# The output projection of a hybrid decoder layer as seven half products, with VectorE alone at the merge and the squares of x1 issued behind the MLP's third column tile

## Chip, cores and metric

One Trainium2 chip, one of its cores. The metric is the device time of one execution in microseconds (us), lower being better. Before the change it is 905.8 us, the median of three runs (905.01 to 906.35). "Engines" are TensorE (PE, with its weight loads as PEld), VectorE (DVE), ScalarE (ACT), GpSimd (POOL) and SyncE (SP), whose queue issues the loads.

## What is computed

One layer for 512 tokens and a width of 1024, all in float32: a chunkwise mLSTM branch (y_a) and a sliding-window attention branch (y_b) on one normalised input, merged by gates, projected and added to x, then an MLP with a squared relu and a gated embedding of the layer's own. The change lies in these lines of the reference:

```python
merged = jax.nn.sigmoid(g_a) * (y_a @ w_branch_a[i]) + jax.nn.sigmoid(g_b) * (y_b @ w_branch_b[i])
x = x + merged @ w_out[i]

u = rmsnorm(x, norm_mlp_g[i]) @ w_up[i]
x = x + jnp.square(jax.nn.relu(u)) @ w_down[i]
```

## The kernel before

**Products.** Every float32 operand is split into a high part (a cast on ACT, L134) and a low part (a subtraction on VectorE, L135; L137 and L138 for columns with a scale), and a product is three matmuls: high with high, high with low, low with high. `chain` (L162) issues them. Weights come by `load_w`: a raw tile of 128x1024 from a ring of four (`wr`), split into rings of four `wh` and `wl`.

**Merge (L846 on).** For each of 8 tiles of 128 columns, TensorE runs 24 matmuls of 128x512 over y_a into a slot `psg` (a ring of two); VectorE multiplies by the gate (L850, `sga`); GpSimd adds the other branch (L851, `gb`); ACT and VectorE split the sum into `mg`. The gates (`gl`) come from DRAM, where an earlier stage has put them, through the SP queue like the weights.

**Output projection (L864 to L897).** The PSUM pool of the first half of the kernel is closed, and a new one (`pq`: three tiles `psp` of two banks, two `psg` of one) is opened; x is loaded into `xk`. For each half of 512 output columns, four loads of w_out with 4 x 6 matmuls each accumulate 128 tokens x 512 columns in four banks: 2 x 96 = 192 matmuls of 128x512. VectorE adds the banks to x (L895). Then `columns_of` (L877) transposes the result x1 in 128x128 pieces, four to a column tile k of 8, and splits each with a scale: this is what the MLP multiplies.

**MLP.** The squares of x1's rows (ACT, L916) and a factor from them (VectorE, L917 and L918) stand in the code ahead of it; the factor is used only when a down product is added to x. An up tile (`up`) is 24 matmuls of 128x512 into `psg`, a relu (L937) and a square (L941) on ACT. A down projection (`down`) already runs as seven half products with sums of quarters, 168 matmuls of 128x512.

A scheduler orders the instructions of each engine from the order of the code and its own costs; on each engine they run in that fixed order, and an instruction that waits holds all that stand behind it on its engine. A tile's next user waits until the earlier users of its slot are done.

Of the kernel before, what the change touches and what calls it, by code (L numbers as in the profile page):

```python
# [22 lines left out]
NEG = -1e30  # L23
NH = 4
DV = 256
# [5 lines left out]
WRB = 4  # L31
LOOK = 2
LMB = 4
# [3 lines left out]
def block_kernel(  # L37
# [39 lines left out]
    wp = pool(ctx, "wp")  # L77
    bp = pool(ctx, "bp")
    ap = pool(st_a, "ap")
    c1 = pool(st_s, "c1", side="right")  # L80
    sp = pool(st_s, "sp", side="right")
    pp = pool(st_p, "pp", space=PSUM)
# [28 lines left out]
    def act_hl(n="s"):  # L111
        return [act_r(n), act_r(n)]

    def big_hl(n):

        hl = [bp.tile([P, KT, 512], F32R, tag="big", bufs=2, name=nm(n)) for _ in range(2)]
        return hl, [[t[:, k, :] for t in hl] for k in range(KT)]

    def tk(n):
        return sp.tile([P, NH * (DV + 1)], F32, tag="tk", bufs=4, name=nm(n))  # L120

    def tok_scratch(n="lm"):
        return sp.tile([P, D], F32, tag="lm", bufs=LMB, name=nm(n))
# [1 line left out]
    def small(n, w, bufs=4):  # L125
        return cp.tile([P, w], F32, tag=f"{n}{w}", bufs=bufs, name=nm(n))
# [4 lines left out]
    def split(dst, src, scale=None):  # L131

        if scale is None:
            A.copy(dst[0], src)  # L134
            V.tensor_sub(dst[1], src, r32(dst[0]))  # L135
        else:
            A.activation(dst[0], src, AF.Copy, scale=scale)  # L137
            V.scalar_tensor_tensor(dst[1], src, scale, r32(dst[0]), ALU.mult, ALU.subtract)  # L138
# [54 lines left out]
    ident = cp.tile([P, P], F32, name="ident")  # L193
# [648 lines left out]
    ya_of(3)  # L842


    mg = []
    for i in range(8):  # L846
        ps = ps_g()
        mm_T(ps, load_w(w_a[i], KT * P, KT), ya)
        sg = act_f("sga")
        V.tensor_mul(sg, ps, gate_of(gad, i))  # L850
        G.tensor_tensor(sg, sg, t2[i], ALU.add)  # L851
        m_ = act_hl("mg")
        split(m_, sg)
        mg.append(m_)


    st_s.close()
    st_p.close()
    xp = pool(ctx, "xp", side="right")
    pp = pool(ctx, "pq", space=PSUM)  # L860
    XK = xp.tile([P, NT, D], F32, name="xk")
    xk = [XK[:, m, :] for m in range(NT)]
    for m in range(NT):
        nc.sync.dma_start(out=xk[m], in_=x[m * P : (m + 1) * P, :])  # L864

    def pair():

        return pp.tile([P, 2, 512], F32, tag="pair", bufs=3, name=nm("psp"))

    def ps_g():  # L870
        return pp.tile([P, 512], F32, tag="g", bufs=2, name=nm("psg"))

    def columns_of(dst, k, g):

        ps = pair()[:, 0, :]
        for m in range(NT):
            T.transpose(ps[:, m * P : (m + 1) * P], xk[m][:, k * P : (k + 1) * P], ident)  # L877
        split(dst[k], ps, g[:, k : k + 1])


    x1b, x1 = big_hl("x1")
    for nh in range(2):
        if nh == 0:
            a, b = pair(), pair()
            pv = [a[:, 0, :], a[:, 1, :], b[:, 0, :], b[:, 1, :]]
        else:
            a = pair()
            pv = [a[:, 0, :], a[:, 1, :], ps_g(), ps_g()]
        for c in range(4):
            w = load_w(w_out[nh * 4 + c], 2 * 512, 2)  # L890
            for m in range(NT):
                mm_tok(pv[m], w, mg[2 * c : 2 * c + 2], m, first=c == 0, last=c == 3)
        for m in range(NT):
            o = xk[m][:, nh * 512 : (nh + 1) * 512]
            V.tensor_add(o, pv[m], o)  # L895
        for k in range(4):
            columns_of(x1, 4 * nh + k, gmlp)  # L897

# [9 lines left out]


    r2 = cp.tile([P, NT], F32, name="r2")
    for m in range(NT):
        junk = np_.tile([P, 7 * 256], F32, tag="uf", bufs=8, name=nm("junk"))[:, :D]
        ss = small("ss", 1)
        A.activation(junk, xk[m], AF.Square, accum_out=ss)  # L916
        V.tensor_scalar(ss, ss, 1.0 / D, EPS, ALU.mult, ALU.add)  # L917
        V.reciprocal(r2[:, m : m + 1], ss)  # L918

    def load_down(q):  # L920
        raws = []
# [9 lines left out]
    def up(q, uf):  # L931
        fs = None
        for f in range(8):
            ps = ps_g()
            mm_T(ps, load_w(w_up[q * 8 + f], KT * P, KT), x1)
            a = mp.tile([P, 512], F32, tag="rt", bufs=3, name=nm("rt"))
            A.activation(a, ps, AF.Relu)  # L937
            if f % 2 == 0:
                fs = F()
            o = 2 * (f % 2)  # L940
            A.activation(fs[:, o : o + 2, :].rearrange("p a b -> p (a b)"), a, AF.Square)  # L941
            if f % 2:
                hl = [np_.tile([P, 7 * 256], F32R, tag="uf", bufs=8, name=nm("uf")) for _ in range(2)]

                cut = 3 * 256 if f == 7 else 0
                if cut:
                    split([t[:, :cut] for t in hl], fs[:, 1:4, :].rearrange("p a b -> p (a b)"))
                V.tensor_add(fs[:, S1, :], fs[:, A21, :], fs[:, A22, :])
                V.tensor_sub(fs[:, S3, :], fs[:, A11, :], fs[:, A21, :])
                V.tensor_sub(fs[:, S2, :], fs[:, S1, :], fs[:, A11, :])  # L950
                V.tensor_sub(fs[:, S4, :], fs[:, A12, :], fs[:, S2, :])  # L951
                split([t[:, cut:] for t in hl], fs[:, 1 + cut // 256 :, :].rearrange("p a b -> p (a b)"))
                uf.append(hl)
# [102 lines left out]

    x2b, x2 = big_hl("x2")
    for k in range(4):
        columns_of(x2, k, gple)
    ple(0, wp0)  # L1060
    for k in range(4, 8):
        columns_of(x2, k, gple)
    evicted = ple(1, load_w(w_pp[1], 2 * 512, 2))
    rk = []
    fs = cp.tile([P, NT, 4], F32, name="fs")
# [113 lines left out]
def _quarters(w):  # L1179


    return w.reshape(2, 2, 2, P, 2, 512).transpose(0, 2, 4, 3, 1, 5).reshape(8, P, 1024)
# [12 lines left out]
def _layout(i):  # L1195
    w = i["w_in"][0]
    down = i["w_down"][0]
    return {
        "x": i["x"][0],
        "p": i["p"][0, 0],  # L1200
        "w_qkml": _t_form(w[:, 0:1024]),
        "w_vml": _quarters(w[:, 1024:2048]).reshape(2, 4, P, 1024).transpose(1, 0, 2, 3).reshape(8, P, 1024),
        "w_o": _t_form(w[:, 2048:3072]),
        "w_vsif": _tok_form(np.concatenate([w[:, 4360:4616], w[:, 3072:3080]], axis=1), KT, 264)[0],
        "w_qsw": _t_form(_heads(w[:, 3080:4104])),
        "w_ksw": _t_form(w[:, 4104:4360]),
        "w_ga": _halves(w[:, 4616:5640]),
        "w_gb": _halves(w[:, 5640:6664]),
        "w_a": _t_form(i["w_branch_a"][0]),
        "w_b": _t_form(_heads(i["w_branch_b"][0].T).T),  # L1210
        "w_out": _tok_form(i["w_out"][0], 2, 512),
        "w_up": _t_form(i["w_up"][0]),
        "w_down": np.concatenate([_quarters(down[q * 1024 : (q + 1) * 1024]) for q in range(4)], axis=0),
        "w_pg": _tok_form(i["w_ple_gate"][0], 2, 512),
        "w_pp": _tok_form(i["w_ple_proj"][0], 2, 512),
        "g_mix": i["norm_mix_g"],
        "g_ml": _columns(i["mlstm_norm_g"][0]),
        "g_mlp": _columns(i["norm_mlp_g"][0]),
        "g_ple": _columns(i["norm_ple_g"][0]),
        "g_fin": i["final_norm_g"][None, :],  # L1220
        "conv": i["conv_qk"][0].reshape(4, KT, P).transpose(2, 1, 0).reshape(P, KT * 4),
        "b_if": i["b_if"],
        "sinks": i["sinks"],
    }
# [19 lines left out]
```

## Time and profile before

| | us |
|---|---|
| median of three runs | 905.8 |
| the profiled run | 905.84 |
| its span | 904.1 |
| TensorE busy | 890.4 |
| VectorE busy | 627.0 |
| ScalarE busy | 466.9 |
| GpSimd busy | 28.1 |

The span is what the trace covers; the rest of the run, 1.7 us, lies outside. Rows of the trace read: start, length, engine, line, operation, out<-in by the program's names without their numbers, form, count, and in brackets the idle time of the engine just before with what ended it. A row of groups gives count, busy us, mean ns of one and the idle time before. Matmuls overlap, so the length of one is more than the step from one to the next.

### The profile page before, as it was taken

Reading aid. Unit: us, or ns where it says so; the run is one execution under the profiler, and the core shown is the slowest. Engines: PE = TensorE matmul, PEld = TensorE weight load, DVE = VectorE, ACT = ScalarE, POOL = GpSimd, SP = SyncE. Lnnn points to the kernel's source line nnn. Section 1 sums busy time; section 2 is a strip of 40 time slices with the busy share of each in tenths; the row PEclk is TensorE's granted clock in tenths of the full one; section 3 lists DMA queues with packets and bytes.
Section 4 is the critical chain, followed back from the end, with each engine's and each line's share of the span. In section 5 each row is a group of like instructions: output and inputs, shape, how many; then the busy total and the mean of one; then the engine's idle time right before and its main releaser. Section 6 shows DMA issues by size and latency. Waiting matters only on the chain.

```text
span 904.1 us, 11781 instructions
## 1 busy us (share of the span) xinstructions
PE 890.4 (98%) x4500; PEld 741.6 (82%) x4500; DVE 627.0 (69%) x1016; ACT 466.9 (52%) x778; POOL 28.1 (3%) x47
## 2 busy tenths in 40 slices
PE   8999999999999999999999999999999999999996
PEld 7888899998877677777878888888888888888786
DVE  6884687874787977557644568856965795689556
ACT  6473444443676667664322555345535543554753
POOL 2021000000000000001210000000000000000000
PEclk9999999999999999999999999999999999999999
DMA  7753134435121132234452620631262044101402
GB/s 259 252 159 125 47 116 157 149 122 168 61 70 52 43 117 71 94 103 150 144 187 94 228 74 2 209 119 45 68 212 94 1 162 161 49 24 50 160 1 94
DMA packets 30347, 101.52 MB, mean 112 GB/s; under 512 B 4301, under 2 KB 4813, under 8 KB 30290
## 3 DMA queue, kind: packets, MB, share of 16 engines
q1 hardware_dynamic: 28002, 93.15, 31.0%
q0 software_dynamic: 2144, 7.35, 2.3%
q8 instruction: 35, 0.57, 0.3%
q10 hardware_dynamic: 144, 0.26, 0.1%
q14 instruction: 22, 0.18, 0.1%
HBM read 91.30 MB, written 8.40 MB: 110 GB/s over the span
## 4 chain that ended last, share of the span: by engine, by line
PE 73%; ACT 2%; DVE 2%; DMA 1%; issue 0%; SPq 0%; ACTq 0%
PE psg L162 42%; PE psp L162 22%; PE pst L784 2%; PE pst L713 1%; PE psa L705 1%; PE pst L774 1%; PE psa L162 1%; PE psa L668 1%; PE psa L669 1%; DMA gfin<-in_g_fin 1%; PE psp L877 1%; ACT jk L796 1%; ACT wh L134 1%; ACT pT L707 0%; DMA ptok<-in_p 0%
## 5 line engine op out<-in xcount | busy, mean ns | idle before, releaser
L135 DVE TENSOR_TENSOR wl<-wr,wh 128x1024 fp32r<-128x1024 f32 x134 | 170.7, 1279 | 131.0 <-ACT wh L134 124.4
L134 ACT CAST wh<-wr 128x1024 fp32r<-128x1024 f32 x134 | 140.9, 1053 | 208.5 <-PE psg L162 85.6
L162 PE MATMUL psg<-x,wh 128*128 128x512 f32 x512 | 157.9, 389 | 0.0
L162 PE MATMUL psp<-wh,uf 128*128 128x512 f32 x448 | 139.2, 390 | 0.0
L162 PEld LDWEIGHTS psg<-x,wh 128*128 128x128 f32 x512 | 96.0, 188 | 19.8
L162 PE MATMUL psg<-h,wh 128*128 128x512 f32 x320 | 101.3, 395 | 0.0
L162 PE MATMUL psg<-x,wl 128*128 128x512 f32 x256 | 99.6, 389 | 0.0
L162 PEld LDWEIGHTS psp<-wh,uf 128*128 128x128 f32 x448 | 84.1, 188 | 17.4
L162 PE MATMUL psp<-wl,uf 128*128 128x512 f32 x224 | 87.2, 390 | 0.0
L134 ACT CAST wh<-wd 128x1024 fp32r<-128x1024 f32 x44 | 46.3, 1055 | 60.4 <-PE psp L162 23.2
L162 PEld LDWEIGHTS psg<-h,wh 128*128 128x128 f32 x320 | 58.7, 188 | 15.9 <-issue 4.9
L135 DVE TENSOR_TENSOR wl<-wd,wh 128x1024 fp32r<-128x1024 f32 x44 | 53.3, 1220 | 17.6 <-ACT wh L134 17.4
L162 PE MATMUL psg<-h,wl 128*128 128x512 f32 x160 | 62.8, 393 | 0.0
L162 PEld LDWEIGHTS psg<-x,wl 128*128 128x128 f32 x256 | 48.1, 188 | 10.0
L162 PE MATMUL psa<-h,wh 128*128 128x256 f32 (+1 forms) x256 | 55.1, 311 | 0.2 <-ACT p L593 0.2
L162 PEld LDWEIGHTS psp<-wl,uf 128*128 128x128 f32 x224 | 42.0, 188 | 8.7
L135 DVE TENSOR_TENSOR uf<-F,uf 128x1792 fp32r<-128x1792 f32 (+2 forms) x20 | 33.0, 1652 | 21.8 <-ACT uf L134 21.8
L162 PEld LDWEIGHTS psa<-h,wh 128*128 128x128 f32 x256 | 41.8, 190 | 3.7 <-ACT p L593 0.9
L162 PE MATMUL psg<-yb,wh 128*128 128x512 f32 x128 | 42.7, 408 | 0.0
L162 PE MATMUL psg<-ya,wh 128*128 128x512 f32 x128 | 40.7, 394 | 0.0
L162 PE MATMUL psa<-h,wl 128*128 128x256 f32 (+1 forms) x128 | 39.6, 309 | 0.0
L134 ACT CAST uf<-F 128x1792 fp32r<-128x1792 f32 (+2 forms) x20 | 28.0, 1399 | 19.3 <-DVE F L951 19.2
(284 smaller groups left out, 1667.7 us busy)
## 6 DMA issues: line engine op xcount, KB each, us to landing
wr<-in_w_up SPq DMA_DIRECT2D x32, 512.0 KB, 3.2
wd<-in_w_down SPq DMA_DIRECT2D x24, 512.0 KB, 3.3
wr<-in_w_o SPq DMA_DIRECT2D x8, 512.0 KB, 4.8
gd<-gr POOLq DMA_DIRECT2D x8, 512.0 KB, 3.2
wr<-in_w_qsw SPq DMA_DIRECT2D x8, 512.0 KB, 4.0
wr<-in_w_qkml SPq DMA_DIRECT2D x8, 512.0 KB, 3.3
wr<-in_w_b SPq DMA_DIRECT2D x8, 512.0 KB, 3.2
gl<-gd SPq DMA_DIRECT2D x8, 512.0 KB, 3.4
```

The lines of the kernel that those rows point to most:

```text
L134: A.copy(dst[0], src)
L135: V.tensor_sub(dst[1], src, r32(dst[0]))
L162: last_mm[0] = T.matmul(ps, l, r, start=first and i == 0, stop=last and i == len(ops) - 1, skip_group_check=parts)
L668: T.matmul(o, q[:, n * P : (n + 1) * P], kk[kp][ab][:, k0 : k0 + 256], start=True, stop=False)
L669: T.matmul(o, q[:, n * P : (n + 1) * P], kl[kp][ab][:, k0 : k0 + 256], start=False, stop=True)
L705: T.transpose(pt[:, c : c + P], lm3[ab][:, g, j * P : (j + 1) * P], ident)
L713: T.matmul(o[HALF[ab], :], vs[n + 1 - nk + j][:, c : c + 64], pTs[j][:, ab * 512 : (ab + 1) * 512], start=j == 0, stop=j == nk - 1,)
L774: T.matmul(psc[:, n0:], qk[4 + h][:, n0 : n0 + P], qk[h][:, n0:], start=True, stop=True)
L784: T.matmul(pn[:, : DV + 1], wT[s][:, t * P : (t + 1) * P], vm[s][:, h, :], start=s == 0, stop=s == t)
L796: A.activation(jk[:, :DV], h_of(h, t), AF.Square, scale=rd[:, t : t + 1], accum_out=hss[:, h, t : t + 1])
L877: T.transpose(ps[:, m * P : (m + 1) * P], xk[m][:, k * P : (k + 1) * P], ident)
```

## The change

- **The matrix of merged columns is not used as it stands, but in quarters.** With the tokens cut into two halves of 256, and the merged columns into even and odd tiles, A11, A21, A12 and A22 are quarters of the merged matrix. For each pair of merge tiles VectorE forms S1 = A21 + A22, S2 = S1 - A11, S3 = A11 - A21, S4 = A12 - S2 (four sums of 128x256). Four tiles are split for each pair: A11 (128x256), A22 with A12, S1 with S2, S3 with S4 (128x512 each).
- **GpSimd's add of the merge is VectorE's** (`V.tensor_add`).
- **w_out is laid out in quarters** b11, b12, b21 and b22 of two tiles each, and VectorE forms their sums (8 operations of 128x1024). b11, b12 are loaded into buffers of the attention stage as these come free, b21 and b22 during the merge. x is loaded into four tiles that held another stage's values, as soon as these come free.
- **Seven half products** of 24 matmuls each: A11, S2, A12, S3, S1, A22, S4, into X and Y (two banks each, `psa`) and Z (two `pst`) of the first PSUM pool; the new pool is opened only afterwards. ACT copies X after A11 (`p_841`, `p_842`), since A11's product is added three times. VectorE makes 14 adds of 128x512 into `xk`, where 8 stood.
- **Columns of x1 come two to a tile** (`two_columns`), two pairs of them set between pieces of the last product.
- **The squares of x1** are issued behind the square of the third up tile.

Where the new order of VectorE differs in the merge: the three rows of each tile before (here two tiles: multiplication by the gate, weight's low part, merged tile's low part; `psg` is the product, `gl` the gate).

```order
L850 TENSOR_TENSOR sga_4097<-psg_4066,gl_4098 128x512
L135 TENSOR_TENSOR wl_4226<-wr_4223,wh_4225 128x1024
L135 TENSOR_TENSOR mg_4103<-sga_4097,mg_4102 128x512
L850 TENSOR_TENSOR sga_4137<-psg_4106,gl_4098 128x512
L135 TENSOR_TENSOR wl_4266<-wr_4263,wh_4265 128x1024
L135 TENSOR_TENSOR mg_4141<-sga_4137,mg_4140 128x512
```

After the change, VectorE between the first pair's adds and the multiplication of the third tile (`sga_4208`, the last row); `ms` holds S1 with S2 (4163) and S3 with S4 (4164), the `wq` sums are quarters of w_out.

```order
L136 TENSOR_TENSOR wl_4307<-wr_4304,wh_4306 128x1024
L136 TENSOR_TENSOR mg_4160<-sga_4152,mg_4159 128x512
L887 TENSOR_TENSOR ms_4163<-sga_4116,sga_4152 128x256
L932 TENSOR_TENSOR wq_4073<-wq_4449,wq_4073 128x1024
L888 TENSOR_TENSOR ms_4163<-ms_4163,sga_4116 128x256
L932 TENSOR_TENSOR wq_4075<-wq_4451,wq_4075 128x1024
L136 TENSOR_TENSOR mg_4168<-ms_4163,mg_4167 128x512
L892 TENSOR_TENSOR ms_4164<-sga_4116 128x256
L893 TENSOR_TENSOR ms_4164<-sga_4152,ms_4163 128x256
L136 TENSOR_TENSOR wl_4363<-wr_4360,wh_4362 128x1024
L136 TENSOR_TENSOR mg_4174<-ms_4164,mg_4173 128x512
L865 TENSOR_TENSOR sga_4208<-psg_4177,gl_4209 128x512
```

A multiplication that followed two rows behind the one of the tile before now stands behind the whole work of the first pair, and behind two weight sums that need loads of b22 (`wq_4449`, `wq_4451`).

ScalarE at the end of the merge after the change: casts of weights (`wh`) and of merged parts (`mg`), and the copies of X (`psa_4459`).

```order
L135 CAST wh_4537<-wq_4453 128x1024
L135 CAST mg_4431<-sga_4426 128x512
L135 CAST wh_4554<-wq_4455 128x1024
L135 CAST mg_4439<-ms_4435 128x512
L135 CAST wh_4573<-wq_4073 128x1024
L135 CAST mg_4445<-ms_4436 128x512
L938 COPY p_841_4499<-psa_4459 128x512
L938 COPY p_842_4500<-psa_4459 128x512
```

The two copies, which before has not, stand behind the cast of the last pair's S3 and S4 (`ms_4436`).

VectorE at the last columns of x1, before: the adds into `xk`, the factor (`ss`, `r`), and the low parts of the last four columns from four tiles `psp`.

```order
L895 TENSOR_TENSOR xk<-psg_4550,xk 128x512
L917 TENSOR_SCALAR ss_4713<-ss_4713 128x1
L918 RECIPROCAL r_4711<-ss_4713 128x1
L917 TENSOR_SCALAR ss_4718<-ss_4718 128x1
L918 RECIPROCAL r_4711<-ss_4718 128x1
L138 SCALAR_TENSOR_TENSOR x_800_4393<-psp_4675,gmlp,x_799_4392 128x512
L138 SCALAR_TENSOR_TENSOR x_800_4393<-psp_4682,gmlp,x_799_4392 128x512
L138 SCALAR_TENSOR_TENSOR x_800_4393<-psp_4689,gmlp,x_799_4392 128x512
```

After the change, the same place: all eight columns (k0, k2, k1, k3, k4, k6, k5, k7), the last two adds, and a weight split.

```order
L139 SCALAR_TENSOR_TENSOR x_832_4458<-psa_4703,gmlp,x_831_4457 128x512
L929 TENSOR_TENSOR xk_4079<-pst_4461,xk_4079 128x512
L139 SCALAR_TENSOR_TENSOR x_832_4458<-psa_4723,gmlp,x_831_4457 128x512
L929 TENSOR_TENSOR xk_4080<-pst_4462,xk_4080 128x512
L139 SCALAR_TENSOR_TENSOR x_832_4458<-psa_4703,gmlp,x_831_4457 128x512
L136 TENSOR_TENSOR wl_4920<-wr_4917,wh_4919 128x1024
L139 SCALAR_TENSOR_TENSOR x_832_4458<-psa_4723,gmlp,x_831_4457 128x512
L139 SCALAR_TENSOR_TENSOR x_832_4458<-psa_4743,gmlp,x_831_4457 128x512
L139 SCALAR_TENSOR_TENSOR x_832_4458<-psa_4756,gmlp,x_831_4457 128x512
L139 SCALAR_TENSOR_TENSOR x_832_4458<-psa_4743,gmlp,x_831_4457 128x512
L139 SCALAR_TENSOR_TENSOR x_832_4458<-psa_4756,gmlp,x_831_4457 128x512
```

Each tile `psa` now appears twice, once for each of its columns; the factor's rows are gone from here, and a weight split for the fourth up tile (`wl_4920`) stands between columns.

The diff, without the deletions of the old loops, which the kernel above shows:

```diff
+    b11 = [load_quarter(4 * kh, sp, "lm", LMB) for kh in range(2)]
+    b12 = [load_quarter(4 * kh + 1, sp, "lm", LMB) for kh in range(2)]
+    xk = [tk("xk")[:, :D] for _ in range(NT)]
+    for m in range(NT):
+        nc.sync.dma_start(out=xk[m], in_=x[m * P : (m + 1) * P, :])
+    def merged(i):
+        ps = ps_g()
+        mm_T(ps, load_w(w_a[i], KT * P, KT), ya)
+        sg = act_f("sga")
+        V.tensor_mul(sg, ps, gate_of(gad, i))
+        V.tensor_add(sg, sg, t2[i])
+        return sg
+    halves_of = lambda t: [t[:, :256], t[:, 256:]]
+    mf = []
+    for i in range(4):
+        even, odd = merged(2 * i), merged(2 * i + 1)
+        a21, a11 = halves_of(even)
+        a22, a12 = halves_of(odd)
...
+        split(part, a11)
...
+        split(hl, odd)
+        V.tensor_add(s1, a21, a22)
+        V.tensor_sub(s2, s1, a11)
...
+        split(hl, t12)
+        V.tensor_sub(s3, a11, a21)
+        V.tensor_sub(s4, a12, s2)
...
+        split(hl, t34)
+    b22 = [load_quarter(4 * kh + 3, wp, "wr", WRB) for kh in range(2)]
+    b21 = [load_quarter(4 * kh + 2, sp, "pT", 2) for kh in range(2)]
+    def halves_a():
+        t = ps_a()
+        return [t[:, :512], t[:, 512:]]
+    def out_proj():
+        X, Y, Z = halves_a(), halves_a(), [ps_t(), ps_t()]
...
+        for kh in range(2):
+            V.tensor_sub(b12[kh], b22[kh], b12[kh])
+        for kh in range(2):
+            prod(X, "A11", form(b11[kh]), kh, True, False)
+            V.tensor_add(b11[kh], b12[kh], b11[kh])
+        own = [act_f("p1") for _ in range(2)]
+        for t in range(2):
+            A.copy(own[t], X[t])
+        for kh in range(2):
+            prod(Y, "S2", form(b11[kh]), kh, True, False)
+        acc(Y, 1, 1)
+        for kh in range(2):
+            prod(X, "A12", form(b21[kh]), kh, False, True)
+            V.tensor_sub(b21[kh], b21[kh], b11[kh])
+        acc(X, 1, 0)
+        for kh in range(2):
+            prod(Y, "S3", form(b12[kh]), kh, False, False)
...
+        for kh in range(2):
+            V.tensor_sub(b11[kh], b22[kh], b11[kh])
+            prod(Z, "S1", form(b11[kh]), kh, True, False)
...
+        for kh in range(2):
+            prod(Y, "A22", form(b21[kh]), kh, False, True)
+        acc(Y, 0, 0)
+        w = [form(b22[kh]) for kh in range(2)]
+        prod(Z, "S4", w[0], 0, False, True)
+        two_columns(0)
+        prod(Z, "S4", w[1], 1, False, True, [0])
+        acc(Z, 1, 1, [0])
+        two_columns(2)
+        prod(Z, "S4", w[1], 1, False, True, [1])
+        acc(Z, 1, 1, [1])
+        two_columns(4)
+        two_columns(6)
+    def two_columns(k):
+        two = halves_a()
+        for i in range(2):
+            columns_of(x1, k + i, gmlp, two[i])
+    out_proj()
...
-    for m in range(NT):
-        junk = np_.tile([P, 7 * 256], F32, tag="uf", bufs=8, name=nm("junk"))[:, :D]
+    def norm_factor():
+        for m in range(NT):
...
-            A.activation(fs[:, o : o + 2, :].rearrange("p a b -> p (a b)"), a, AF.Square)
+            squared = A.activation(fs[:, o : o + 2, :].rearrange("p a b -> p (a b)"), a, AF.Square)
+            if (q, f) == (0, 2):
+                with tc.issue_after(squared.ins):
+                    norm_factor()
```

More of the change, by code (lines that the diff above doesn't have):

```diff
@@ L79, in block_kernel @@
     ap = pool(st_a, "ap")
+    xp = pool(ctx, "xp", side="right")
     c1 = pool(st_s, "c1", side="right")
@@ L119, in tk @@
     def tk(n):
-        return sp.tile([P, NH * (DV + 1)], F32, tag="tk", bufs=4, name=nm(n))
+        return xp.tile([P, NH * (DV + 1)], F32, tag="tk", bufs=4, name=nm(n))
     def tok_scratch(n="lm"):
@@ L842, in block_kernel, with load_quarter @@
     ya_of(3)
-    mg = []
-    for i in range(8):
+    def load_quarter(c, pool_, tag, bufs):
+        t = pool_.tile([P, 1024], F32, tag=tag, bufs=bufs, name=nm("wq"))
+        nc.sync.dma_start(out=t, in_=w_out[c])
+        return t
+    b11 = [load_quarter(4 * kh, sp, "lm", LMB) for kh in range(2)]
[4 more added lines that the diff above has]
+    def merged(i):
         ps = ps_g()
@@ L850, in block_kernel @@
         V.tensor_mul(sg, ps, gate_of(gad, i))
[L851 to L854, printed above, removed]
+        V.tensor_add(sg, sg, t2[i])
[6 more added lines that the diff above has]
+        a22, a12 = halves_of(odd)
+        if i % 2 == 0:
+            own = act_hl("mg")
+        part = [halves_of(t)[i % 2] for t in own]
+        split(part, a11)
+        f = {"A11": part}
+        hl = act_hl("mg")
+        split(hl, odd)
+        f["A22"], f["A12"] = zip(*[halves_of(t) for t in hl])
+        t12, t34 = act_f("ms"), act_f("ms")
+        s1, s2 = halves_of(t12)
+        s3, s4 = halves_of(t34)
+        V.tensor_add(s1, a21, a22)
+        V.tensor_sub(s2, s1, a11)
+        hl = act_hl("mg")
+        split(hl, t12)
+        f["S1"], f["S2"] = zip(*[halves_of(t) for t in hl])
+        V.tensor_sub(s3, a11, a21)
+        V.tensor_sub(s4, a12, s2)
+        hl = act_hl("mg")
+        split(hl, t34)
+        f["S3"], f["S4"] = zip(*[halves_of(t) for t in hl])
+        mf.append(f)
@@ new lines, in block_kernel, with columns_of, form, prod @@
+    b22 = [load_quarter(4 * kh + 3, wp, "wr", WRB) for kh in range(2)]
[3 more added lines that the diff above has]
+        return [t[:, :512], t[:, 512:]]
+    def columns_of(dst, k, g, ps):
+        for m in range(NT):
+            T.transpose(ps[:, m * P : (m + 1) * P], xk[m][:, k * P : (k + 1) * P], ident)
+        split(dst[k], ps, g[:, k : k + 1])
+    def out_proj():
+        X, Y, Z = halves_a(), halves_a(), [ps_t(), ps_t()]
+        def form(raw):
+            return load_w(None, 1024, 2, raw)
+        def prod(ps, a, w, kh, first, last, toks=range(2)):
+            for t in toks:
+                ops = []
+                for k in range(2):
+                    ops += pairs([h[:, t * P : (t + 1) * P] for h in mf[2 * kh + k][a]], [h[:, k, :] for h in w])
+                chain(ps[t], ops, first and kh == 0, last and kh == 1, True)
+        def acc(ps, toks, n, part=range(2)):
+            for t in part:
+                o = xk[2 * toks + t][:, n * 512 : (n + 1) * 512]
+                V.tensor_add(o, ps[t], o)
+        for kh in range(2):
[15 more added lines that the diff above has]
+            prod(Y, "S3", form(b12[kh]), kh, False, False)
+        acc(Y, 0, 1)
+        acc(own, 0, 1)
+        for kh in range(2):
+            V.tensor_sub(b11[kh], b22[kh], b11[kh])
+            prod(Z, "S1", form(b11[kh]), kh, True, False)
+        acc(Z, 0, 1)
+        acc(own, 1, 1)
+        acc(own, 0, 0)
+        for kh in range(2):
[11 more added lines that the diff above has]
+        two_columns(6)
@@ L857, in block_kernel @@
+    x1b, x1 = big_hl("x1")
+    def two_columns(k):
[3 more added lines that the diff above has]
+    out_proj()
     st_s.close()
     st_p.close()
-    xp = pool(ctx, "xp", side="right")
     pp = pool(ctx, "pq", space=PSUM)
-    XK = xp.tile([P, NT, D], F32, name="xk")
-    xk = [XK[:, m, :] for m in range(NT)]
-    for m in range(NT):
-        nc.sync.dma_start(out=xk[m], in_=x[m * P : (m + 1) * P, :])
     def pair():
@@ L871, in ps_g @@
         return pp.tile([P, 512], F32, tag="g", bufs=2, name=nm("psg"))
[L873 to L897, printed above, removed]
     st_a.close()
@@ L912, in block_kernel @@
     r2 = cp.tile([P, NT], F32, name="r2")
-    for m in range(NT):
-        junk = np_.tile([P, 7 * 256], F32, tag="uf", bufs=8, name=nm("junk"))[:, :D]
[L915 to L918, printed above, removed]
+    def norm_factor():
+        for m in range(NT):
+            junk = np_.tile([P, 7 * 256], F32, tag="uf", bufs=8, name=nm("junk"))[:, :D]
+            ss = small("ss", 1)
+            A.activation(junk, xk[m], AF.Square, accum_out=ss)
+            V.tensor_scalar(ss, ss, 1.0 / D, EPS, ALU.mult, ALU.add)
+            V.reciprocal(r2[:, m : m + 1], ss)
     def load_down(q):
@@ L1058, in block_kernel @@
     for k in range(4):
-        columns_of(x2, k, gple)
+        columns_of(x2, k, gple, pair()[:, 0, :])
     ple(0, wp0)
     for k in range(4, 8):
-        columns_of(x2, k, gple)
+        columns_of(x2, k, gple, pair()[:, 0, :])
     evicted = ple(1, load_w(w_pp[1], 2 * 512, 2))
@@ L1210, in _layout @@
         "w_b": _t_form(_heads(i["w_branch_b"][0].T).T),
-        "w_out": _tok_form(i["w_out"][0], 2, 512),
+        "w_out": _quarters(i["w_out"][0]),
         "w_up": _t_form(i["w_up"][0]),
```

## The prediction, made before the changed kernel ran

> **What bounds the kernel now.** The first view is the page's busy times with the line of granted clock, the second the chain of work that ended last, in order of time, around the change (columns: start, length, engine, what, how many).
>
> ```profile
> span 904.1 us, 11781 instructions
> PE 890.4 (98%) x4500; PEld 741.6 (82%) x4500; DVE 627.0 (69%) x1016; ACT 466.9 (52%) x778; POOL 28.1 (3%) x47
> PEclk9999999999999999999999999999999999999999
> ```
>
> ```profile
> 419.41 39.87 PE psg L162 x174
> 459.30 1.05 ACT wh L134
> 460.37 22.03 PE psp L162 x96
> 506.25 1.44 PE psp L877 x12
> 510.43 41.31 PE psg L162 x182
> 551.74 38.08 PE psp L162 x168
> 589.82 43.52 PE psg L162 x192
> ```
>
> TensorE is busy 98% of the span, and the chain runs along it: the merge to 459.3, one step of 1.05 us off it, then the output projection and the MLP. 192 matmuls of 128x512 take 43.52 us, so one is 0.2267 us. The 168 of a down projection take 38.08, the same 0.2267: seven products already run elsewhere in this kernel without a wait. So a matmul removed here is worth its full 0.2267, and each new wait of TensorE costs in full. The waits of TensorE from 410 to 760 show how little idle time there is to win:
>
> ```profile
> PE psp L162 <- ACT wh L134: 0.9, 1, 0.9
> ```
>
> **What goes.** 192 matmuls become 168: 24 x 0.2267 = 5.44 us. The wait between merge and projection goes too: the chain has it as 459.30 to 460.37, 1.07 us. There the new PSUM pool could not be written until VectorE had read the last merge tile; the row blames ACT, but the cast begins before that read ends. In the change the projection starts in slots of the old pool that have long been free, with weights already split. From 460.37 to 510.43 the chain holds 50.06 us, in which TensorE issues 202 matmuls (192 and ten of the first up tile) and 32 transposes. At 0.2267 and, by 1.44/12, 0.12 us, these make 49.6; some 0.5 is small gaps around transposes. I count the new tail gap by gap, so the 0.5 goes as well. Removed: 5.44 + 1.07 + 0.5 = 7.0 us.
>
> **What VectorE gets in the merge.** Groups of the merge by line, VectorE then GpSimd (columns: busy us, mean ns, idle before), and behind them single rows of VectorE and GpSimd.
>
> ```profile
> L135 DVE TENSOR_TENSOR wl<-wr,wh 128x1024 fp32r<-128x1024 f32 x8 | 16.3, 2038 | 1.1 <-ACT wh L134 1.1
> L850 DVE TENSOR_TENSOR sga<-psg,gl 128x512 f32<-128x512 f32 x8 | 5.5, 690 | 9.7 <-PE psg L162 9.7
> L851 POOL TENSOR_TENSOR sga<-sga,gb 128x512 f32<-128x512 f32 x7 | 9.9, 1419 | 238.3 <-ACT wh L134 223.5 <-DVE sga L850 14.8
> ```
>
> ```profile
> 454.91 1.28 POOL L851 TENSOR_TENSOR sga<-sga,gb 128x512 f32<-128x512 f32 x1 [4.20 <-ACT wh L134]
> 454.95 2.33 DVE L135 TENSOR_TENSOR wl<-wr,wh 128x1024 fp32r<-128x1024 f32 x1 [0.17 <-ACT wh L134]
> 457.20 0.68 DVE L135 TENSOR_TENSOR mg<-sga,mg 128x512 fp32r<-128x512 f32 x1
> 549.16 0.42 DVE L949 TENSOR_TENSOR F<-F 128x256 f32<-128x256 f32 x1
> 549.50 1.22 DVE L986 TENSOR_TENSOR wd<-wd,wd 128x1024 f32<-128x1024 f32 x1
> 558.23 1.22 DVE L997 TENSOR_TENSOR wd<-wd,wd 128x1024 f32<-128x1024 f32 x1
> 559.36 1.22 DVE L135 TENSOR_TENSOR wl<-wr,wh 128x1024 fp32r<-128x1024 f32 x1
> ```
>
> A 1024 wide subtraction takes 1.22 us, started every 1.13 to 1.14; a 512 wide one 0.68, every 0.60; a 256 wide one 0.42, every 0.34 (549.16 to 549.50). In the merge the 1024 wide one takes 2.04 on average, and the row of 2.33 begins together with GpSimd's add of 1.28. With that add gone I take 1.14. The other end is 2.04, in case the stage and not the add lengthens it; it makes the slower rival. [...]
>
> Between the merge's first multiplication and the last split of S3 and S4 the new order gives VectorE 8 multiplications, 8 adds and 12 splits of 512, four splits and 16 sums of 256, and 16 operations of 1024: 28 x 0.60 + 20 x 0.34 + 16 x 1.14 = 41.8 us, in the 46 or so from 423.7 to 470. VectorE is now 90% full there, and delays come from the order:
>
> - Merge tile 4 needs the PSUM slot of tile 2, whose multiplication stands behind all work of the first pair. Counting back from 459.30 in steps of 24 x 0.2267 = 5.44, tile 1 ends at 426.7 and tile 3 at 437.5. From 426.7 VectorE has a multiplication, two 512s, a 1024 and two 256s (3.7 us, to 430.4), then a weight sum with the first quarter of b22, a 256, and a sum that waits for the second quarter.
>
> ```profile
> 429.27 6.62 SPq L143 DMA_DIRECT2D wr<-in_w_out  x2
> wr<-in_w_out SPq DMA_DIRECT2D x8, 512.0 KB, 3.3
> xk<-in_x SPq DMA_DIRECT2D x4, 512.0 KB, 5.4
> ```
>
> That load is issued when the split at about 429.9 frees its buffer (before issues one at 429.27) and lands 3.3 us later, at 433.2. Behind it stand two 1024s, two 512s and two 256s, 4.2 us; tile 2's multiplication ends near 438.1, and tile 4 starts **0.7 late** (0 if the load lands a microsecond sooner; 2.8 if it takes x's 5.4).
> - A12 adds into the bank of A11, which ACT copies first. The copies stand behind the cast of S3 and S4 of the last pair. With tile 7 ending at 460.0, S2 ends at 470.9. VectorE's split of the first b21 waits for ACT's cast, and this for A11's first half: 464.0. From there three 1024s, two 512s and four 256s, 6.0 us, so S4 ends at 470.1; a cast of 0.62 and two copies of 0.59 (row below) later it is 471.9. **1.0 late**, with 0 to 2 as bounds. The other five products have their splits 0.1 us or more ahead.
>
> **The tail.** Columns of x1 now use a two-bank tile for two columns, and the second column's transposes wait for the first column's split. The rows show one round, near the kernel's end:
>
> ```profile
> 842.02 0.59 ACT L1054 COPY pe<-psg 128x512 f32<-128x512 f32 x1 [0.68 <-PE psg L162]
> 843.52 0.75 DVE L138 SCALAR_TENSOR_TENSOR x<-psp,gple,x 128x512 fp32r<-128x512 f32 x1
> 844.33 0.66 PE L877 MATMUL psp<-ident,xk 128*128 128x128 f32 x4 [0.54 <-DVE x L138]
> 845.02 0.69 ACT L137 ACTIVATE x<-psp,gple 128x512 fp32r<-128x512 f32 x1 [0.46 <-PE psp L877]
> 845.59 0.66 PE L877 MATMUL psp<-ident,xk 128*128 128x128 f32 x4 [0.60 <-DVE x L138]
> 846.28 0.69 ACT L137 ACTIVATE x<-psp,gple 128x512 fp32r<-128x512 f32 x1 [0.57 <-PE psp L877]
> 847.00 0.75 DVE L138 SCALAR_TENSOR_TENSOR x<-psp,gple,x 128x512 fp32r<-128x512 f32 x1 [0.16 <-ACT x L137]
> ```
>
> Transposes to ACT 0.69 (844.33 to 845.02), ACT to VectorE 0.72 (846.28 to 847.00), VectorE 0.75, and 0.06 until the next transposes (843.52 + 0.75 to 844.33): 2.2 us a round. With P the end of S4's first half, four transposes 0.45 and the matmuls in their places, the columns start at: k0 P, k2 1.8, k1 3.2, k3 4.1, none late. k4 needs k1's split, which VectorE does behind the last add of x: 5.7 instead of 4.5. Behind k1's split stands a weight split of 1024, whose cast also precedes ACT's half of k3, so k6 starts at 7.6, k5 at 8.2, k7 at 9.8, and the first up tile at 10.2. Without waits it would be 12 x 0.2267 + 32 x 0.113 = 6.3: **3.9 late**. Bounds: 1.7 if the weight split and the add were not in the way (two bare rounds), 6 if a second weight split came between. Nothing covers these 3.9: only transposes and the up tile behind them are left. Moving the squares of x behind the third up tile delays only ACT's next relu by some 4 us; its PSUM slot is needed 5.44 later, so I cost that at nothing, and a microsecond if the cover fails.
>
> **Sum.** 905.84 (the profiled run, 1.7 outside its span; the median is 905.8) - 7.0 + 0.7 + 1.0 + 3.9 = 904.4.
>
> **Rivals.**
> - *The tail hides.* The trace has rounds only where ACT and VectorE were nearly free; if the adds and weight split run earlier than I walk them, 1.7 or less is left: 902.2, or 900.5 with no tail wait. Against it: the order of the two queues is fixed.
> - *VectorE becomes the bound of the merge (slower).* The 41.8 us fill 46; the 16 long operations decide. Above 1.14 + 4.5/16 = 1.42 us each every further microsecond is TensorE's. At 1.65 (between 1.14 and 2.04) it is 3.7 more: 908.1; at 2.04, 914. For it: the mean of 2038 ns; against it: 1.22 wherever GpSimd rests.
> - *Loads collide.* x and half of w_out now come before and during the merge, when gates for the last columns of y_a are due:
>
> ```profile
> 415.00:420.00 5.00, 5.00 (x30) 4.18 (x28) 4.68 (x7) 1.66 (x3) 0.00 (x0) 1.00 0.91 313
> 840.00:845.00 5.00, 4.45 (x23) 3.33 (x21) 2.54 (x5) 3.10 (x6) 0.00 (x0) 1.00 0.89 324
> ```
>
> The share of DMA is 0.91 there already (the last two columns are share and GB/s, the one ahead the clock). A load at 5.4 instead of 3.3 would cost up to 2 us: 905.4 to 906.4. For the forecast: x is issued some six microseconds earlier.
> - *The clock drops in the tail.* At half clock the tail's 6.3 and the up tile's 5.4 double: 916. Against it: from 840 to 845 TensorE waits twice for rounds, and the clock stays 1.00. [...]
>
> **How the numbers follow.** Forecast 904.4 (902.9 to 906, tail from 2.4 to 5.5) 0.46; tail hidden 0.21; collision 0.09; VectorE bound 0.22; clock 0.02. A measurement of this kernel tells about 0.2% from no change, 1.8 us: faster is below 904.0, slower above 907.6. Of the forecast's 0.46, 0.18 lies below 904.0. Faster 0.18 + 0.21 = 0.39; same 0.28 + 0.09 = 0.37; slower 0.24. The range of 8 in 10 reaches from the hidden tail to VectorE's mid price: 900.5 to 908.5.
>
> **What would show it.** Right: 168 matmuls at 0.2267, 1024 wide splits in the merge at 1.22, TensorE waiting 0.7 on the multiplication at merge tile 4, 1.0 on ACT's copies, about 3.9 on splits of x1. Wrong: waits at every merge tile, a gate or quarter that lands late, more than one weight split between two columns, or waits in the first up tiles.

## The result, and the profile after

The changed kernel takes 907.94 us (median of 17 runs, 905.45 to 910.38) where the kernel before takes 905.24 (17 runs beside them, 904.39 to 906.37): a ratio of 1.0026, 95% interval 1.0019 to 1.0033. By that ratio it is slower by some 2.4 us. The time lies in the range of the prediction, but on the other side of the kernel before from the forecast of 904.4. That the range holds it is luck: its upper end was priced with VectorE as the bound of the merge, which did not happen.

The profiled run took 908.09 with a span of 906.3, 2.2 more than before. The page's busy times and its line of granted clock:

```profile
span 906.3 us, 11792 instructions
PE 887.3 (98%) x4476; PEld 737.4 (81%) x4476; DVE 654.2 (72%) x1072; ACT 476.8 (53%) x794; POOL 16.8 (2%) x39
PEclk9999999999999999999999899999999999999999
```

TensorE issues 24 matmuls fewer, but is busy only 3.1 us less, not 5.4, and one digit of the clock is an 8, which the page of before does not have: slice 23, 498 to 521 us. TensorE's waits from 410 to 760, and the chain around the change:

```profile
PE psa L909 <- DVE x L139: 2.5, 3, 1.1
PE psg L163 <- DVE sga L865: 1.7, 1, 1.7
PE pst L825 <- DVE sy L826: 0.6, 2, 0.4
PE psa L163 <- ACT p L938: 0.4, 1, 0.4
```

```profile
429.32 4.59 DMA wq<-in_w_out
438.92 22.04 PE psg L163 x96
494.67 2.74 PE pst L163 x12
504.81 1.13 PE psa L909 x4
508.61 45.03 PE psg L163 x192
553.63 38.08 PE psp L163 x168
```

The places named in the prediction are all there: the fifth merge tile behind VectorE's multiplication (1.7), A12 behind ACT's copies (0.4, and some 0.7 of smaller gaps in the products), the columns of x1 behind VectorE's splits. New is the last row but one: 192 up matmuls take 45.03 us, where before they take 43.52. The view by stretches of time shows why (columns: PE, PEld, DVE, ACT and POOL busy, the granted clock, DMA share, GB/s):

```profile
500.00:505.00 5.00, 3.05 (x18) 1.89 (x17) 5.00 (x8) 3.28 (x5) 0.00 (x0) 0.98 0.76 264
505.00:510.00 5.00, 4.29 (x16) 3.60 (x16) 2.55 (x4) 2.06 (x3) 0.00 (x0) 0.50 0.95 356
510.00:515.00 5.00, 5.00 (x20) 4.00 (x20) 1.34 (x2) 0.00 (x0) 0.00 (x0) 0.84 0.54 220
```

From 504.8 to 511.6 the granted clock is half. Before, it is full in every microsecond until TensorE's work is done (its last matmul ends at 897.2, and the clock falls at 899.7). The timeline of TensorE there:

```profile
501.70 0.66 PE L909 MATMUL psa<-ident,xk 128*128 128x128 f32 x4
503.11 0.63 PE L909 MATMUL psa<-ident,xk 128*128 128x128 f32 x4 [0.74 <-DVE x L139]
504.81 1.97 PE L909 MATMUL psa<-ident,xk 128*128 128x128 f32 x8 [1.07 <-DVE x L139]
507.49 1.12 PE L909 MATMUL psa<-ident,xk 128*128 128x128 f32 x4 [0.71 <-DVE x L139]
508.26 1.20 PE L163 MATMUL psg<-x,wh 128*128 128x512 f32 x2
509.26 0.63 PE L163 MATMUL psg<-x,wl 128*128 128x512 f32 x1
511.74 0.39 PE L163 MATMUL psg<-x,wl 128*128 128x512 f32 x1
```

Four transposes take 0.63 at 503.1 and 1.12 at 507.5; a matmul of the up tile 0.63 at 509.3 and 0.39 from 511.7.

Against the prediction's sum (all from this profile; 497.23 is where the columns start, P):

| term | forecast | measured |
|---|---|---|
| 24 matmuls, the wait at the end of the merge, small gaps | -7.0 | -7.0 |
| fifth merge tile | +0.7 | +1.7 |
| products: 438.92 + 22.04 to 497.41, less 156 x 0.2267 | +1.0 | +1.1 |
| tail: 497.23 to 508.26, less 6.3 | +3.9 | +4.7, of it 0.9 by the half clock |
| first up tile at half clock, 45.03 - 43.52 | 0 | +1.5 |
| y_a behind its gates (0.6, before 0.2) | 0 | +0.4 |
| sum | -1.4 | +2.4 (spans: +2.2) |

The first row is the forecast's count, taken over as it stands. The 0.9 is an estimate against `filled_tail` below, which runs the same columns at full clock: the four transposes whose split k7 waits for take 1.13 us here and 0.66 there, and from k7's first transpose to the first up matmul it is 0.77 here and 0.35 there. So the clock costs some 2.4 us: 0.9 in the tail and 1.5 in the up tile.

### The profile page after: what moved, and what is told of

Read it like the earlier page. It is cut to its first block, busy times and chain, and to the rows that moved or that the text cites. A ratio compares the mean times of both kernels' runs of the same rounds, so it can differ in the third digit from the quotient of the medians.

```text
span 906.3 us, 11792 instructions
## 1 busy us (share of the span) xinstructions
PE 887.3 (98%) x4476; PEld 737.4 (81%) x4476; DVE 654.2 (72%) x1072; ACT 476.8 (53%) x794; POOL 16.8 (2%) x39
## 4 chain that ended last, share of the span: by engine, by line
PE 90%; DVE 4%; DMA 3%; ACT 2%; issue 1%; SPq 0%; ACTq 0%; DVEq 0%
PE psg L163 48%; PE psp L163 19%; PE psa L163 12%; PE pst L163 2%; PE pst L785 2%; PE pst L714 1%; PE psa L706 1%; PE pst L775 1%; PE psa L669 1%; PE psa L670 1%; DVE wl L136 1%; DMA wr<-in_w_vsif 1%; DMA gfin<-in_g_fin 1%; DVE x L139 1%; ACT jk L797 1%
## 5 line engine op out<-in xcount | busy, mean ns | idle before, releaser
L136 DVE TENSOR_TENSOR wl<-wr,wh 128x1024 fp32r<-128x1024 f32 x126 | 153.2, 1222 | 111.4 <-ACT wh L135 101.3
L135 ACT CAST wh<-wr 128x1024 fp32r<-128x1024 f32 x126 | 132.2, 1051 | 180.0 <-PE psg L163 72.3
L135 ACT CAST wh<-wq 128x1024 fp32r<-128x1024 f32 x26 | 27.4, 1053 | 35.9 <-PE psg L163 18.4
```

## The experiments

The theory at the start: TensorE's new waits cost what the table says, and those of the tail cost more than themselves, because the idling lowers the granted clock for some 7 us. Its rivals: something else lowers the clock (the load burst at a DMA share of 0.95 stands at the same place); VectorE is simply too full, so that any wait taken away comes back; the add on VectorE or the place of the squares is the cost. Each run's kernel before was timed on the same chip and took 905.5 to 905.9; beside the changed kernel it took 905.24, so differences of half a microsecond between runs mean nothing. All but `vector_add_alone` edit the changed kernel.

**Filled tail.** Small matmuls that nobody reads, in four groups between the last columns:

```diff
         for i in range(2):
+            if k > 2:
+                for _ in range(5):
+                    tc.keep_in_program_order(T.matmul(fill[:, :256], mf[0]["A11"][0][:, :P], mf[0]["S1"][0], start=True, stop=True))
             columns_of(x1, k + i, gmlp, two[i])
```

> The changed kernel with four groups of five small matmuls more (128x256, never read) between the last columns of x1, where TensorE waits. Theory that idling lowers the clock: the columns come when ACT and VectorE let them, as in the change, but the clock stays near 1.00, so the transposes and the first up tile are not stretched: 1.5 to 2.3 us less than the change, 905.6 to 906.4, with more work on TensorE. Rival (loads or something else lower the clock): clock 0.5 again and no gain, 907.9 or a little more.

Measured: 906.25 (11 runs, 905.06 to 907.53), 1.7 less than the change, with more work. The same stretches, and the chain's row for the up tiles:

```profile
500.00:505.00 5.00, 4.02 (x28) 3.23 (x27) 5.00 (x8) 3.36 (x5) 0.00 (x0) 1.00 0.36 107
505.00:510.00 5.00, 5.00 (x33) 4.34 (x34) 2.63 (x4) 2.04 (x3) 0.00 (x0) 1.00 0.94 356
```

```profile
507.81 43.55 PE psg L163 x192
```

The clock stays at 1.00 although the loads run at the same 356 GB/s from 505 to 510; TensorE is busy for 4.02 of the 5 us ahead of that, where the change has 3.05. So here the idling lowered it, not the loads. From k0's first transpose to the end of the 192 up matmuls it is 54.1 us (497.29 to 551.36) where the change has 56.4 (497.23 to 553.64): 2.3 less, near the estimate of 2.4. It is not the profiled execution alone: the mean granted clock of a whole run is 0.993 to 0.997 in the 17 runs of the change, and 0.996 to 0.999 in the 11 of `filled_tail` and in the 23 of before beside them.

**Tiles of their own.** Each column of x1 gets a PSUM tile for itself:

```diff
-        two = halves_a()
         for i in range(2):
-            columns_of(x1, k + i, gmlp, two[i])
+            columns_of(x1, k + i, gmlp, ps_g() if i else ps_a()[:, :512])
```

> Every column of x1 has a PSUM tile of its own (psa and psg in turn), so no column waits for its neighbour's split. Theory of waits and clock (the two columns of one tile wait for each other, TensorE idles, and the granted clock falls to half from about 505 to 511 us): TensorE waits less than 1 us in the tail instead of 2.5, the clock stays 1.00, the first up tile is back at 5.4 us; about 4.5 us less than the change, 903.4 (902.5 to 904.5). Rival (VectorE's queue is what is late in the tail, whoever owns the tiles): about 1 us less, 907. Second rival (the clock falls with the burst of loads there, not with the idling): the waits go and the clock falls all the same, 905.5.

Measured: 908.09 (907.65 to 909.76), no gain at all. The waits view (first row) and single microseconds of the clock:

```profile
PE psg L163 <- DVE x L139: 3.2, 1, 3.2
```

```profile
505.00:506.00 1.00, 0.00 (x0) 0.00 (x0) 0.99 (x2) 1.00 (x3) 0.00 (x0) 1.00 0.96 332
507.00:508.00 1.00, 0.00 (x0) 0.00 (x0) 1.00 (x2) 0.08 (x1) 0.00 (x0) 1.00 0.98 250
508.00:509.00 1.00, 0.84 (x2) 0.75 (x3) 0.10 (x1) 0.00 (x0) 0.00 (x0) 0.59 0.98 348
511.00:512.00 1.00, 1.00 (x5) 0.81 (x4) 0.00 (x0) 0.00 (x0) 0.00 (x0) 0.70 1.05 426
512.00:513.00 1.00, 1.00 (x6) 0.82 (x5) 0.00 (x0) 0.00 (x0) 0.00 (x0) 1.00 1.00 410
```

Neither the theory's number nor the rivals' reason fits at once: the columns no longer wait, but the first up tile waits 3.2 us in one piece. The reading: the new pool's first `psg` lies on the old pool's `psg` banks, and those now hold the last columns until VectorE has split them. Behind these 3.2 us without a matmul the clock is half for about 3.4 us (by the rows, 508.18 to 511.60). The next run tests the reading.

**Banks apart.** Only k1 and k3 on the `psg` banks, k4 to k7 on `psa` and `pst`:

```diff
+            ps = ps_a()[:, :512] if i == 0 else ps_g() if k < 4 else ps_t()
+            columns_of(x1, k + i, gmlp, ps)
```

> Like the run with tiles of their own, but the last columns of x1 (k4 to k7) use the two psa and the two pst tiles, and only k1 and k3 the psg banks, on which the first up tile is put next. Theory (in the run with own tiles the wait went from the columns to the first up tile only because that tile takes a psg bank that VectorE had not yet read): no wait over 0.5 us from the last product to the first up tile, clock 1.00 throughout, 192 up matmuls in 43.5 us; 4.5 to 6 us less than the change, 902 to 903.5. Rival (VectorE and ACT are too late with the columns in any case): a wait of 2 us or more on splits of x1 inside the first up tile, and the clock low again, above 906.

Measured: 902.74 (901.75 to 903.82), 2.8 under the kernel before (ratio 0.997, interval 0.9958 to 0.9982) and 5.2 under the change. The tail has one wait left (0.7, where the expectation allowed 0.5), the clock is 1.00 there, and the up tiles run at full pace:

```profile
PE psa L909 <- DVE xk L929: 0.7, 1, 0.7
```

```profile
503.46 43.55 PE psg L163 x192
```

**b22 early.** b22 and b21 exchange buffers, so that the weight sums with b22 leave the merge's first pair:

```diff
-    b22 = [load_quarter(4 * kh + 3, wp, "wr", WRB) for kh in range(2)]
-    b21 = [load_quarter(4 * kh + 2, sp, "pT", 2) for kh in range(2)]
+    b22 = [load_quarter(4 * kh + 3, sp, "pT", 2) for kh in range(2)]
+    b21 = [load_quarter(4 * kh + 2, wp, "wr", WRB) for kh in range(2)]
```

> b22 and b21 exchange buffers (b22 into the attention stage's two, b21 into two of the weight ring). The two weight sums with b22 then no longer stand in the first pair of the merge. Theory (the load of b22 holds VectorE's queue, and with it the third tile's multiplication and the fifth merge tile): the 1.7 us wait goes, 906.2 (905.8 to 906.8). Rival (VectorE is too full in the merge anyway): the wait moves to a later tile, less than 0.5 us won. If b21 lands late in the weight ring, A12 waits instead.

Measured: 907.88 (12 runs, 905.5 to 909.09), the time of the change, not the 906.2 of the theory. The wait at the fifth merge tile is gone, and another has come:

```profile
PE psa L163 <- ACT wh L135: 1.5, 2, 1.0
```

The last clause of the expectation is what happened: b21 comes late in the weight ring. The run does not tell whether the sums' place matters; the next does.

**Sums later.** The loads as in the change, the two sums behind the fourth tile's multiplication:

```diff
-        V.tensor_mul(sg, ps, gate_of(gad, i))
+        muls.append(V.tensor_mul(sg, ps, gate_of(gad, i)))
...
         for kh in range(2):
-            V.tensor_sub(b12[kh], b22[kh], b12[kh])
+            with tc.issue_after(muls[3].ins):
+                V.tensor_sub(b12[kh], b22[kh], b12[kh])
```

> The two weight sums with b22 are issued behind the multiplication of the fourth merge tile instead of inside the first pair, loads and buffers as in the change. Theory (VectorE's queue, held by the load of b22, makes the fifth merge tile late): the 1.7 us wait goes and nothing takes its place; 1.5 to 1.9 us less than the change, 906.2. Rival (VectorE is full in the merge, so what is moved comes back): waits of together 1 us or more at later merge tiles or the first products, 907.5.

Measured: 906.59 (11 runs, 905.43 to 908.49), 1.35 less than the change, a little under the 1.5 to 1.9 expected. By times alone this is weak: the ratios to the kernels before are 1.0014 (1.0005 to 1.0022) and 1.0026 (1.0019 to 1.0033). The trace is plain. Waits on `sga` are gone from the view, nothing of that size replaces them, and TensorE is busy without a gap in the merge (20 of 20 us between 425 and 445, where the change has 18.27). VectorE was not too full; its queue was held by a load (for 2.29 us, to 433.93, in the change). The half clock of the tail is still there, for 3.4 us in this profile.

**Banks and sums.** Both edits.

> Both edits together: no wait at the fifth merge tile, none in the columns, clock 1.00. If the two places are independent, the gains add: 900.5 to 902, which is 3 to 5 us under the kernel before. If not, about that of the better one alone, 902 to 903.5.

Measured: 901.61 (900.91 to 902.24), ratio to the kernel before 0.9956 (0.9944 to 0.9968): 3.9 us faster than before, 6.3 faster than the change. All waits of TensorE from 410 to 760:

```profile
PE psa L911 <- DVE xk L931: 0.7, 1, 0.7
PE psa L163 <- ACT p L941: 0.3, 1, 0.3
PE pst L825 <- DVE sy L826: 0.2, 1, 0.2
```

The two gains against the change, 5.2 and 1.35, add up to 6.55, so the places are independent within the runs' scatter. Against `banks_apart`, timed beside it and also at full clock, the sums' place gains 1.1.

**The add, in three runs.** `vector_add_alone` is the kernel before with its one line `G.tensor_tensor(sg, sg, t2[i], ALU.add)` as `V.tensor_add(sg, sg, t2[i])`; `gpsimd_add` and `best_gpsimd_add` are the opposite edit in the changed kernel and in the one with both edits.

> The kernel before with one edit: the merge's add on VectorE instead of GpSimd. Theory (the add on GpSimd and the 1024 wide split shut each other out): the eight splits of the merge fall from 2.0 to 1.22 us, VectorE is no busier than before, TensorE keeps its pace there: the time of the kernel before within 0.5 us. Rival (the add costs VectorE's path): the wait at the end of the merge grows by 0.6 us or more.

> The add of the merge back on GpSimd, all else as changed. Theory that GpSimd's add and VectorE's two-input operations shut each other out: the 1024 wide splits beside an add take about 2.2 us again, and VectorE, with eight more of its operations per pair than before, falls behind: more than 1.7 us of wait at the fifth merge tile and new ones behind it, 909 to 912. Rival (the add on VectorE is itself a cost): its 0.6 us less per tile shortens the waits by about 1 us, 907.

> The kernel with both edits, with the merge's add back on GpSimd. Theory of the lock: splits beside an add take 1.8 us or more, VectorE is late with the merge's last pair and TensorE waits for A11's and S2's operands as in the changed kernel with that add: 1 to 2 us slower, 902.6 to 903.6. Rival (the add's place does not matter): 901.6 within 0.4.

Measured: 905.69 against 905.92 before (interval of the ratio 0.999 to 1.0007), so no difference; 909.06 (907.6 to 910.07), 1.1 over the change; 902.43 (901.56 to 903.4), 0.8 over the kernel with both edits and just under the 902.6 to 903.6 expected. VectorE's splits in the merge of `vector_add_alone`, then of `best_gpsimd_add` with GpSimd's add:

```profile
L135 DVE TENSOR_TENSOR wl<-wr,wh 128x1024 fp32r<-128x1024 f32 x8 | 9.7, 1217 | 0.0
```

```profile
L136 DVE TENSOR_TENSOR wl<-wr,wh 128x1024 fp32r<-128x1024 f32 x4 | 8.2, 2042 | 0.3 <-ACT wh L135 0.3
L868 POOL TENSOR_TENSOR sga<-sga,gb 128x512 f32<-128x512 f32 x8 | 13.0, 1625 | 244.9 <-ACT wh L135 216.6 <-DVE sga L867 28.3
```

With GpSimd's add the split takes 2.04 us on average in the kernel before and in `best_gpsimd_add` and 1.77 in `gpsimd_add`, without it 1.22 in `vector_add_alone` and in the change: the add and not the stage lengthens it. Rows of `best_gpsimd_add` in order of time show that the add is lengthened too:

```profile
439.37 1.22 DVE L935 TENSOR_TENSOR wq<-wq,wq 128x1024 f32<-128x1024 f32 x1
439.60 2.14 POOL L868 TENSOR_TENSOR sga<-sga,gb 128x512 f32<-128x512 f32 x1 [1.64 <-DVE sga L867]
440.51 2.31 DVE L136 TENSOR_TENSOR wl<-wr,wh 128x1024 fp32r<-128x1024 f32 x1
```

The weight sum that starts first keeps its 1.22; the add that starts during it takes 2.14, where others of this run take 1.29; and the split that starts during the add takes 2.31 instead of 1.22.

Taking the add to VectorE costs nothing in the kernel before. That it gains with seven products is not shown by the times, whose ratios to the kernels before are 0.9956 (0.9944 to 0.9968) without GpSimd's add and 0.996 (0.9947 to 0.9974) with it; the profile with it has two new waits of 0.6 us, on a split of a weight and on a multiplication by the gate. `gpsimd_add` missed its expectation in one part: its wait at the fifth merge tile is 1.5, not more than 1.7; new waits of the products on splits of weights and merged tiles (0.6 and 0.4) came.

**The squares, in two runs**: the call of `norm_factor` back in the code ahead of the MLP, in the changed kernel and in the one with both edits.

> The changed kernel with the squares of x1 where they stood before (in the code ahead of the MLP). Expected from the prediction's cost of nothing for their move: within 0.7 us of the change if ACT has room there, 907.2 to 908.6. Rival (the four squares of 1.05 us stand between the last columns on ACT): the columns' waits grow by 1 to 4 us and the clock stays low longer, 909 to 913; then the move of the squares is worth that much.

> The kernel with both edits (banks apart, sums later), with the squares of x1 back in the code ahead of the MLP; on ACT three of them then stand between the columns k3 and k4. Theory (ACT has no room in the tail once TensorE does not wait there): k4 is split some 3 us later, the first up tile waits 1.5 to 3 us for it, and the clock may fall: 903 to 905. Rival (their place is worth nothing, as the prediction had it and as the changed kernel with its long tail waits showed): 901.6 within 0.5.

Measured: 907.0 (12 runs, 904.23 to 909.66), a little under the 907.2 expected, and 901.68 (900.91 to 902.27) against 901.61. The squares fill ACT between the columns without delaying the first up tile: it comes 10.3 us behind P in `squares_first`, where the change has 11.0, and 7.1 behind P in `best_squares_first`, as in `banks_apart`. The theory of the second run fell. Their place is worth nothing that these runs can tell.

## Why the prediction was wrong, step by step

- **What goes: held.** 168 matmuls run at 0.2267 us where the clock is full, and the wait of 1.07 us at the end of the merge is gone.
- **Fifth merge tile: right place and reason, wrong size (0.7 forecast, 1.7 measured).** The chain shows the load of the second b22 quarter issued at 429.32 and awaited until 433.9: 4.6 us, not the 3.3 of the median row, so it landed 0.7 later than the walk's 433.2. VectorE's work behind it took what was counted (4.2 us, from 433.93 to the multiplication's start at 438.08). Tile 3 ended 0.3 earlier than counted back. A range to 2.8 was given, but the sum used 0.7. `sums_later` confirms the reason.
- **A12 behind ACT's copies: right place, and a sum that fits in part by luck.** All gaps of the products are 1.1 against 1.0, but the wait on the copies is only 0.4 of it; the rest is smaller gaps that the sum put at nothing.
- **Tail's waits: held.** 3.8 us without the clock's estimated part, against 3.9; the weight split between the columns is there as walked. `banks_apart` shows that they were due to two columns sharing a tile: there the tail is 7.1 us (496.09 to 503.22), 0.8 over the 6.3.
- **The clock: the step that failed.** The prediction named this rival and gave it 2 in 100, on the ground that from 840 to 845 TensorE waits for two rounds and the clock stays 1.00. So the sum held no term for it, and it cost some 2.4 us. The two waits were of 0.54 and 0.60, and TensorE was busy for 2.27 of the 3.41 us around them (842.20 to 845.61); the tail's walk had waits of 1.4 and 1.1 close together in it, and in the change TensorE is busy there for 1.47 of 3.41 us (501.39 to 504.80). No stretch of before is as thin (the thinnest, from 306.3, has 1.80 of 3.41) until its end, where the clock does fall, 2.5 us behind the last matmul. The rival's price was also too high: not the whole tail and tile at half clock (11.7 us), since the half clock began late in the tail and ended after 6.8 us. In `own_tiles` the clock fell right after one wait of 3.2 us without a matmul. The change has no single wait over 1.1 us in its tail and its clock fell too, so the length of one gap does not decide it there.
- **VectorE as the bound of the merge: did not happen.** Of the two ends that the prediction weighed for the 1024 wide split, the traces show the short one once GpSimd's add is gone: a mean of 1.22 us in the merge of the change and of `vector_add_alone`, 2.04 in the kernel before with the add.
- **Loads that collide:** 0.4 us at most. y_a waits 0.6 for its gates in the profile of the change and 0.2 in that of `sums_later`, whose loads at that place are the same, so part of it may be scatter.

Without the clock's 2.4 us and the tile's extra microsecond the table's sum would be -1.0, on the forecast's side; `filled_tail`, which takes away only the first, is at the kernel before's time (ratio 1.0007, interval 0.9999 to 1.0016).

## What to carry to other kernels

Where a serial chain of short rounds puts several waits of TensorE close together, price the clock with them: in this kernel some 3.8 us of waits cost 2.4 more by half clock, and the mark of the place was a stretch of 3.41 us with TensorE busy for less than half of it (1.47). When tiles are rearranged to take a wait away, look at which banks the next stage opens on: in `own_tiles` the wait returned there in one piece of 3.2 us. And an operation that waits for a load belongs behind those that free a buffer for TensorE: moving two sums by a few places on VectorE's queue was worth 1.1 to 1.35 us.

## What the runs showed of the hardware that was not expected

The granted clock by single microseconds, in the change:

```profile
503.00:504.00 1.00, 0.63 (x4) 0.42 (x4) 1.00 (x1) 0.58 (x2) 0.00 (x0) 1.00 0.84 324
504.00:505.00 1.00, 0.19 (x1) 0.19 (x2) 1.00 (x3) 0.46 (x1) 0.00 (x0) 0.90 1.04 397
505.00:506.00 1.00, 1.00 (x6) 1.00 (x6) 0.41 (x1) 0.04 (x1) 0.00 (x0) 0.50 0.99 406
```

Read as full clock for 0.8 us and half clock for 0.2, the mean of 0.90 puts the fall at 504.80. Read in the same way, the clock rises at 511.62 (0.69 from 511 to 512) and falls next at 904.16 (0.58 from 904 to 905), behind the end of TensorE's work. In `own_tiles` it falls at 508.18 (0.59 from 508 to 509) and rises at 511.60 (0.70 from 511 to 512).

**In all six profiles whose tail has it, half clock lasts about 3.4 us or twice that**: 6.82 in the change and 6.8 in `b22_early`; 3.42 in `own_tiles` and in `sums_later`, 3.40 in `squares_first` and 3.4 in `gpsimd_add`. For `b22_early` and `gpsimd_add` this is read from stretches of 5 us, for the others from single microseconds.

Stretches of 3.41 us ahead of a fall, behind one, and around other waits show how much TensorE was busy:

| run | stretch, us | TensorE busy, of 3.41 us | clock in the stretch | clock after it |
|---|---|---|---|---|
| after | 501.39 to 504.80 | 1.47 | full | half |
| after | 504.80 to 508.21 | 2.69 | half | half |
| after | 508.21 to 511.62 | 3.41 | half | full |
| after | 436.53 to 439.95 | 1.70 | full | full |
| after | 897.33 to 900.74 | 1.58 | full | full |
| sums_later | 499.17 to 502.59 | 2.4 | full | full |
| sums_later | 502.59 to 506.00 | 1.59 | full | half |
| before | 306.30 to 309.71 | 1.80 | full | full |
| before | 842.20 to 845.61 | 2.27 | full | full |

In these rows, of the stretches at full clock, half clock follows those with 1.47 and 1.59 us and none with 1.70 or more, but full clock follows the one with 1.58 at the end of the change; full clock comes back after the stretch at half clock with 3.41 and not after the one with 2.69. These figures are read off afterwards; no run set out to move a stretch across them. The merge's one wait of 1.7 us (1.70 busy) did not lower the clock. `filled_tail` and `banks_apart`, with TensorE busy for 4.02 and 4.29 of the 5 us from 500 to 505 where the change has 3.05, keep full clock there.
